# A three-block transformer forward pass: order of the first loads and splits, and identity products in TensorE's foreseen waits

## The chip, the core and the metric

The kernel runs on one core of a Trainium2 chip. The metric is the device time of one execution in microseconds (us), shown as the median of several runs. TensorE is the matrix engine (PE in the profile, PEld for its weight loads), VectorE is DVE, ScalarE is ACT, GpSimd is POOL, and SyncE (SP) issues most transfers.

## What is computed

The input x has 256 tokens of 2048 features, all in float32. A first block is a mixture of three mixers, cross attention to 256 memory tokens, and a feed-forward part with a short convolution; a second part has two layers. In outline:

```python
proj = h @ w_in                      # split into s5, stick-breaking and sparse-attention inputs
y = concat(s5_mixer(u5), stick_breaking(sq, sk, sv), nsa_mixer(nq, kc, vc, ksl, vsl, ksw, vsw, g))
h = layer_norm(ALPHA * h + y @ w_out)
h = layer_norm(ALPHA * h + memory_cross_attention(h, mem))
h = layer_norm(ALPHA * h + conv_ffn(h))
...
# second part, two layers
x = x + mixer(rmsnorm(x))            # latent attention and pooling, then a short convolution
x = x + square(relu(rmsnorm(x) @ w_mlp_up)) @ w_mlp_down
```

Nearly all the arithmetic is in products of a 256-token activation with weight matrices that are read once from memory. The change concerns the very first of them, `h @ w_in`, and the places where TensorE waits.

## The kernel before, in words

**Main products.** `plan` is a list of entries. An entry is a group of weights, mostly 4 rows of 128 by 512 columns (1 MB), loaded by SP into one of three buffers `raw`. To keep float32 precision, each weight group is split in two halves of 1024 columns: ScalarE writes the rounded part to `whi` (`split_hi`), VectorE the rest to `wlo` (`split_lo`). The activation is split in the same way into a tile `rt` of 512 columns, high part and low part for 256 tokens. TensorE then does one product of `whi` with all 512 columns, and one of `wlo` with 256, for each 128 by 128 block of weights (`blocks`). The results land in PSUM tiles called `bank`. Small tensors of the mixers live in one large tile `ft` (some in `st`), cut into buffers by `buf`.

**Order of work.** The program text of each engine is written in Python by a planner. The main products are emitted in the order of `plan`; side work (transposes, set-up of the mixers, attention heads, normalisation) is written as generators ("threads") that the planner advances between the main products. It does so by a clock of its own: `spent` adds the planned cost of each operation to a clock per engine (`clk`), and keeps for each 32-column block of a tile the planned time of the last write and the last read (`region`). A thread is advanced when its time has come by the planned TensorE clock. `B.side(gen, t)` adds a thread with a due time `t` in ns; `turn_cols` has 40000 and the set-up of the sparse attention (`nsa.setup`) 45000. `copy_out`, `scale_rows` and `vt` choose an engine by these clocks, and `Arena.get` the place of a buffer.

**The start.** `network` emits the first loads. `load_consts` loads all constants (1004 columns, identity first) from ACT's queue. The loop over four chunks of x (256 tokens by 512 features each, 0.5 MB) loads chunk 0 from SP's queue and chunks 1 to 3 from ACT's, and weight groups 0 to 2 from SP's. A one-column copy on POOL reads chunk 2, and POOL's own loads and its chain of small operations for the S5 mixer stand behind that copy. Then `load_cols` issues some fifteen small loads of parameter columns from SP's queue; the next weight group is loaded by SP after these. `run` first splits two half groups (`self.ahead(2)`); `start`, called before the first entry, adds the threads, among them `trans` for the four chunks: it transposes each 128-feature piece on TensorE and splits it with ScalarE and VectorE into an `rt` tile.

**Names.** `identr` is a 128 by 128 identity in the rounded format; it serves already to add terms to a bank (`extra` in `blocks`). `mixfree` is the list of banks that side work may take; the main products have banks of their own (`lin`).

Of the kernel before, what the change touches and what calls it, by code (L numbers as in the profile page):

```python
# [70 lines left out]
CBIG, COFF, COH = _consts()  # L71
# [10 lines left out]
NCOL = _o  # L82
# [18 lines left out]
DEPTH = 6  # L101
MARGIN = 0.0
ORDER = "u5 sq sk kv nq0 nq1 g sv h0 h1 ksl units ksw"
W = "waits"
READ = "read"

# [146 lines left out]
class Builder:  # L253
# [5 lines left out]
    def __init__(self, tc, I, out):  # L259
        self.tc, self.I, self.out = tc, I, out  # L260
        self.nc = Engines(tc.nc, self)
        self.clk = dict(pe=0.0, dve=0.0, act=0.0, pool=0.0, qsync=0.0, qact=0.0, qpool=0.0, dma=0.0)
        self.times = {}
        self.table = None
        self.cur = None
        self.plan = []
        self.queue = []
        self.depth = DEPTH
        self.spawned = []
        self.persist = 0  # L270
        self.evacs, self.reading = None, {}
        self.quiet = 0


    def act(self, out, in_, func=AF.Copy, scale=1.0, bias=0.0, accum=None):
# [122 lines left out]
    def bank(self):  # L398
        while not self.mixfree:
            yield W  # L400
        return self.mixfree.popleft()

    def keep_bank(self, has=lambda: False):

        while not has() and (not self.mixfree or self.persist >= max(1, 8 - self.nlin - 2)):
            yield W
        if has():
# [29 lines left out]
    def spent(self, key, name, a, kw):  # L437
        outs = [kw[k] for k in ("out", "accum_out") if kw.get(k) is not None] or [a[0]]
        ins = [x for x in list(a) + list(kw.values()) if hasattr(x, "shape") and hasattr(x, "dtype") and not any(x is o for o in outs)]
        n = max([_free(x) for x in outs + ins])  # L440
        pointers = sum(_free(x) == 1 for x in ins) if n > 1 else 0
        end = LAT
        if name == "dma_start":
            if key == "pool":

                self.clk["pool"] += 1000.0
                self.clk["qpool"] = max(self.clk["qpool"], self.clk["pool"] + 1000.0)

            key, c = "q" + key, 450.0
            size = max(outs[0].shape[0], ins[0].shape[0]) * n * 4 / 360.0  # L450
        elif key == "pe":
            end = 60.0
            c = _free(outs[0])
            if name == "transpose":
                c = 0.84 * c
            elif ins[-1].dtype == FR:
                c = c / 2.4 + 14.1
            else:
                c = max(c * 1.667, 26)
        elif key == "act":  # L460
            c = 92 + 0.84 * n + 93 * pointers
            s = TABLE.get(kw.get("func"))
            if s and s != self.table:
                self.table = s
                c += 1300.0
        elif key == "pool":
            c = 120 + 3.5 * n if name == "tensor_copy" else 150 + (0.74 if name == "affine_select" else 2.1) * n
        elif name in ("tensor_scalar", "tensor_copy"):
            c = 64 + 0.52 * n + 62 * pointers
        else:  # L470
            c = 66 + 1.05 * n * (8 if name == "reciprocal" and n > 16 else 1) + 60 * pointers
        t = self.clk[key]
        ri = [x for x in map(self.region, ins) if x is not None]
        ro = [x for x in map(self.region, outs) if x is not None]
        for w, r in ri:
            t = max(t, w.max())
        for w, r in ro:
            t = max(t, r.max(), 0 if key == "pe" or name == "dma_start" else w.max())
        self.clk[key] = t + c
        self.lastc = c  # L480
        if name == "dma_start":
            self.clk["dma"] = max(self.clk["dma"], t + 1000) + size
            c, end = self.clk["dma"] - t, 1500.0
        f = t + c + end
        for w, r in ri:
            np.maximum(r, f - 60, out=r)
        for w, r in ro:
            w[:] = f
        if self.cur is not None:
            self.cur.t = max(self.cur.t, f)  # L490

    def ready(self, ap):
        return self.region(ap)[0].max()

    def step(self, th):

        was, self.cur = self.cur, th
        try:
            r = next(th.gen) or True
            th.steps = 99 if r is READ else th.steps + (r is not W)  # L500
            return r
# [250 lines left out]
    def run(self):  # L752
        self.halves = [(i, j) for i, e in enumerate(self.plan) for j in range(e.nhalf)]
        self.nhi = self.nlo = self.nhalf = 0
        self.ahead(2)
        for i, e in enumerate(self.plan):
            for f in e.before:
                f()
            self.consume(i)
        self.flush()  # L760
# [38 lines left out]

    def load_consts(self):  # L800
        nc = self.nc
        self.cb = self.buf(CBIG.shape[1], True)
        nc.scalar.dma_start(out=self.cb.ap, in_=self.I["cbig"])
        nc.vector.tensor_copy(out=self.identr, in_=self.cst("ident"))
        self.ones = self.buf(128, True)
        nc.vector.memset(self.ones.ap, 1.0)
        self.small = self.buf(8)
        for i, v in enumerate((1.0 / 2048, 1.0 / 512, 1.0 / 192, 1.0 / 1536, math.pi / 2)):
            nc.vector.memset(self.small.ap[:, i:i + 1], v)
        self.halfpi = self.small.ap[:, 4:5]  # L810
        nc.vector.memset(self.small.ap[:, 5:7], 0.0)
        for h in range(2):
            nc.vector.memset(self.small.ap[h * 64:h * 64 + 64, 5 + h:6 + h], 1.0 / 192)
# [5 lines left out]
    def load_cols(self):  # L819

        nc = self.nc
        self.pcol = self.buf(NCOL, True)
        nt = (NCOL + 127) // 128
        st = self.buf(nt * 128)
        sv = st.v(nt)
        for name, rows in COLS:
            src = self.I[name]
            names = " ".join(f"a{i}" for i in range(len(src.shape)))
            flat = src.rearrange(f"{names} -> ({names})") if len(src.shape) > 1 else src
            flat = flat.rearrange("(r c) -> r c", c=128)  # L830
            r = 0
            while r < rows:
                g = COL0[name] + r
                t, p = divmod(g, 128)
                m = min(rows - r, 128 - p)
                nc.sync.dma_start(out=sv[p:p + m, t], in_=flat[r:r + m])
                r += m
        def turn():
            for t0 in (0, 4):
                b = yield from self.bank()  # L840
                n = min(512, NCOL - t0 * 128)
                for t in range(t0, min(t0 + 4, nt)):
                    m = min(128, NCOL - t * 128)
                    nc.tensor.transpose(b[:, (t - t0) * 128:(t - t0) * 128 + m], sv[0:m, t], self.cst("ident")[0:m, 0:m])
                yield
                self.act(self.pcol.ap[:, t0 * 128:t0 * 128 + n], b[:, 0:n])
                self.unbank(b)
                yield
            st.free()
            self.hb = self.buf(4)  # L850
            c = COL0["s5_b_glu"]
            self.ts(self.hb.ap, self.pcol.ap[:, c:c + 4], 0.5, ALU.mult)
            yield
        self.turn_cols = turn
# [1658 lines left out]
def block1(B, dpool):  # L2513
    nc, I = B.nc, B.I
# [9 lines left out]
    stg = {}  # L2524

    def stage(n, c):
        stg[n, c] = B.buf(1024)
        (nc.scalar if n == "x" and c else nc.sync).dma_start(out=stg[n, c].v(2), in_=I[n][0, :, c * 512:(c + 1) * 512].rearrange("(t p) f -> p t f", p=128))
        return stg[n, c]

    def trans(n, c, lin=False):
# [30 lines left out]
    RT = 0.9  # L2562

    def start():
        B.side(s5.setup())
        for c in range(4):
            B.side(trans("x", c), B.ready(stg["x", c].ap))
        B.side(B.turn_cols(), 40000.0)
        B.side(nsa.setup(), 45000.0)
# [94 lines left out]
    def units():  # L2664
        B.side(nsa.biases(), prio=2)
        for h in range(16):
            for br in range(2):
                B.side(nsa.unit(h, br), prio=3)
    for n in ORDER.split():
        if n == "units":  # L2670
# [268 lines left out]
def network(tc, I, out, es):  # L2939
    B = Builder(tc, I, out)  # L2940
    nc = B.nc
    dpool = es.enter_context(tc.tile_pool(name="dr", bufs=1, space=bass.MemoryType.DRAM))
    B.setup(es)
    B.load_consts()
    stage, s5, nsa, e = block1(B, dpool)
    block2(B, e)
    s5.load_rows()
    for c in range(4):
        x = stage("x", c)
        if c < B.NRAW:  # L2950
            B.load(c)
        if c == 2:

            t = B.buf(1)
            nc.gpsimd.tensor_copy(out=t.ap, in_=x.ap[:, 0:1])
    s5.load()
    nsa.load()
    B.load_cols()
    B.negones = B.buf(128)
    nc.vector.memset(B.negones.ap, -1.0)  # L2960
    gen_setup(B)
    B.run()
    return B
# [27 lines left out]
```

## Time and profile before

| | us |
|---|---|
| median of 3 runs | 3513.49 |
| the runs | 3511.28 to 3513.76 |
| profiled execution, whole | 3515.05 |
| its span, first to last instruction | 3513.3 |
| TensorE busy in the span | 3426.3 (98%) |
| VectorE busy | 2371.4 (67%) |
| ScalarE busy | 1725.5 (49%) |
| GpSimd busy | 215.7 (6%) |
| mean granted TensorE clock | 0.989 of full speed |

A busy TensorE is not always one at its peak: its products overlap and their ends are modelled. The granted clock has two levels, 1.00 (2.4 GHz) and 0.50 (1.2 GHz); a value between them is a mean over a stretch that has both. All instructions that the planner emits through its wrappers carry one line number, L233, so groups are told apart by the tiles they write and read.

### The profile page before, as it was taken

How to read it: one execution, taken by the hardware profiler on the slowest of the kernel's cores; microseconds unless marked ns; L12 is line 12 of the kernel's file. 1: busy time of each engine (PE TensorE's matmuls, PEld its weight loads, DVE VectorE, ACT ScalarE, POOL GpSimd, SP SyncE). 2: the span in 40 equal slices, each digit the busy share in tenths (PEclk: the TensorE clock that was granted, in tenths of full speed). 3: DMA queues.
4: the chain of work that ended last, by engine and by line, in shares of the span. 5: the costliest groups of instructions: out<-in, count | busy, mean ns of one | idle time of the engine just before them, and what ended most of it. 6: DMA issues, size and time to landing. Idle time of an engine off the chain costs nothing.

```text
span 3513.3 us, 49562 instructions
## 1 busy us (share of the span) xinstructions
PE 3426.3 (98%) x19448; PEld 2940.8 (84%) x19448; DVE 2371.4 (67%) x3978; ACT 1725.5 (49%) x2652; POOL 215.7 (6%) x319
## 2 busy tenths in 40 slices
PE   8998999899999999999999999999999999999999
PEld 6777688788888887787888888888888888888887
DVE  4977677876676578877765656567666664656565
ACT  4445645555455455654544444444454544434343
POOL 4001010001000001000000000000221000000001
PEclk8999999999999999999999999999999999999999
DMA  5452244355555555443555555555555555555554
GB/s 181 132 166 96 56 168 165 134 192 188 187 191 192 187 186 167 150 126 126 170 190 192 188 186 189 192 180 192 184 189 191 192 191 186 187 191 192 186 187 143
DMA packets 323779, 605.15 MB, mean 172 GB/s; under 512 B 18843, under 2 KB 36243, under 8 KB 323545
## 3 DMA queue, kind: packets, MB, share of 16 engines
q1 hardware_dynamic: 319609, 596.91, 51.5%
q10 hardware_dynamic: 3264, 4.19, 0.5%
q8 instruction: 152, 2.49, 0.3%
q0 software_dynamic: 672, 0.89, 0.1%
q14 instruction: 82, 0.67, 0.1%
HBM read 599.26 MB, written 2.69 MB: 171 GB/s over the span
## 4 chain that ended last, share of the span: by engine, by line
PE 87%; DVE 10%; issue 1%; ACT 1%; POOL 1%; DMA 1%; ACTq 0%; SPq 0%; DVEq 0%; POOLq 0%
PE bank L233 87%; DVE ft L233 6%; DVE wlo L233 3%; POOL ft L233 1%; DVE rt L233 0%; ACT ft L233 0%; DMA ft<-in_x_dram 0%; ACT whi L233 0%; DMA raw<-in_w_in_dram 0%; DMA raw<-in_even_w_ukv_dram 0%; DMA raw<-in_even_w_uq_dram 0%; POOL st L233 0%; DVE st L233 0%; ACT rt L233 0%; ACT L284 0%
## 5 line engine op out<-in xcount | busy, mean ns | idle before, releaser
L233 PE MATMUL bank<-rt,whi 128*128 128x512 f32 (+1 forms) x8784 | 2785.7, 399 | 47.6 <-DVE ft L233 27.3
L233 PEld LDWEIGHTS bank<-rt,wlo 128*128 128x128 f32 (+1 forms) x8784 | 1651.7, 189 | 388.8 <-DVE wlo L233 0.4
L233 DVE TENSOR_TENSOR wlo<-raw,whi 128x1024 fp32r<-128x1024 f32 x1134 | 1379.2, 1222 | 719.6 <-ACT whi L233 717.1
L233 ACT ACTIVATE whi<-raw 128x1024 fp32r<-128x1024 f32 x1134 | 1189.4, 1050 | 1344.3 <-PE bank L233 1271.5
L233 PE MATMUL bank<-rt,wlo 128*128 128x256 f32 (+1 forms) x8784 | 1727.8, 279 | 0.0
L233 PEld LDWEIGHTS bank<-rt,whi 128*128 128x128 f32 (+1 forms) x8784 | 1347.6, 189 | 79.6 <-DVE ft L233 28.9
L233 DVE TENSOR_TENSOR ft<-bank,ft 128x256 f32<-128x256 f32 (+2 forms) x879 | 358.3, 420 | 286.7 <-ACT ft L233 198.5
L233 POOL TENSOR_TENSOR ft<-ft 128x256 f32<-128x256 f32 (+1 forms) x179 | 149.1, 844 | 2912.8 <-DVE ft L233 2061.4
L233 ACT ACTIVATE ft<-bank 128x256 f32<-128x256 f32 (+3 forms) x499 | 190.4, 392 | 189.7 <-PE bank L233 161.1
L233 PE MATMUL bank<-ft 128*128 128x128 f32 (+9 forms) x1073 | 213.5, 346 | 33.9 <-DVE ft L233 21.8
L233 DVE SCALAR_TENSOR_TENSOR ft<-ft 128x256 f32<-128x256 f32 (+2 forms) x441 | 225.8, 513 | 13.0 <-ACT ft L233 2.5
L233 PEld LDWEIGHTS bank<-ft 128*128 128x128 f32 (+4 forms) x1073 | 137.6, 171 | 87.6 <-DVE ft L233 25.4
L233 ACT ACTIVATE ft<-ft 128x256 f32<-128x256 f32 (+3 forms) x365 | 165.8, 467 | 90.4 <-DVE ft L233 70.1
L233 DVE TENSOR_TENSOR ft<-ft 128x256 f32<-128x256 f32 (+4 forms) x463 | 194.1, 442 | 14.1 <-ACT ft L233 8.7
L233 ACT ACTIVATE rt<-ft 128x256 fp32r<-128x256 f32 x317 | 138.6, 439 | 85.2 <-DVE ft L233 80.3
L233 DVE TENSOR_TENSOR rt<-ft,rt 128x256 fp32r<-128x256 f32 x220 | 91.7, 445 | 5.2 <-ACT rt L233 5.2
L233 PE MATMUL bank<-whi,rt 128*128 128x256 f32 (+1 forms) x320 | 80.6, 329 | 1.4 <-DVE ft L233 1.4
L233 ACT ACTIVATE ft<-ft,st 128x256 f32<-128x256 f32 (+1 forms) x146 | 64.5, 464 | 19.3 <-DVE st L233 18.5
L233 PEld LDWEIGHTS bank<-whi,rt 128*128 128x128 f32 x320 | 55.5, 190 | 7.6 <-ACT whi L233 1.2
L233 PE MATMUL bank<-wlo,rt 128*128 128x256 f32 (+1 forms) x160 | 52.1, 326 | 0.0
L233 DVE SCALAR_TENSOR_TENSOR rt<-ft,rt 128x256 fp32r<-128x256 f32 x97 | 45.1, 475 | 0.3 <-ACT rt L233 0.3
L233 ACT ACTIVATE rt<-bank 128x256 fp32r<-128x256 f32 x56 | 20.0, 380 | 45.0 <-PE bank L233 44.9
(76 smaller groups left out, 464.9 us busy)
## 6 DMA issues: line engine op xcount, KB each, us to landing
raw<-in_w_mlp_up_dram SPq DMA_DIRECT2D x128, 1024.0 KB, 5.3
raw<-in_w_mlp_down_dram SPq DMA_DIRECT2D x128, 1024.0 KB, 5.1
raw<-in_ffn_w_up_dram SPq DMA_DIRECT2D x88, 1024.0 KB, 5.0
raw<-in_odd_w_in_dram SPq DMA_DIRECT2D x48, 1024.0 KB, 5.2
raw<-in_ffn_w_down_dram SPq DMA_DIRECT2D x44, 1024.0 KB, 5.1
raw<-in_w_in_dram SPq DMA_DIRECT2D x36, 1024.0 KB, 5.1
raw<-in_w_out_dram SPq DMA_DIRECT2D x16, 1024.0 KB, 5.1
raw<-in_even_w_in_dram SPq DMA_DIRECT2D x16, 1024.0 KB, 5.4
```

The lines of the kernel that those rows point to most:

```text
L233: return f(*a, **kw)
```

## The change

1. Constants: only the identity (128 columns) is loaded first, from ACT's queue; the other 876 columns follow from SP's queue after chunk 2 of x and weight group 2. All four chunks of x are loaded from SP's queue.
2. Splits: `self.ahead(2)` moves from `run` into `start`, behind the transposes and splits of chunk 0, which are emitted at once and not as a thread.
3. Buffers: the constants, the parameter columns and the one-column buffer get widths that are multiples of 32.
4. `warm`: when the planner's clock says that TensorE will wait 1400 ns or more for the operands of its next operation (`KEEP`), products of the identity with itself, 128 by 512, are emitted ahead of that operation, one for each 227 ns of the foreseen wait less 600 ns (`KEPT`). They write the first bank of `mixfree` whose planned use has ended; where there is none, none is emitted. The planner's clocks don't count them.

```diff
@@ -101,6 +101,9 @@
 DEPTH = 6
 MARGIN = 0.0
 ORDER = "u5 sq sk kv nq0 nq1 g sv h0 h1 ksl units ksw"
+
+KEEP = 1400.0
+KEPT = 600.0
 W = "waits"
 READ = "read"
 
@@ -270,6 +273,7 @@
         self.persist = 0
         self.evacs, self.reading = None, {}
         self.quiet = 0
+        self.peend, self.nwarm = 0.0, 0
 
 
     def act(self, out, in_, func=AF.Copy, scale=1.0, bias=0.0, accum=None):
@@ -476,6 +480,9 @@
             t = max(t, w.max())
         for w, r in ro:
             t = max(t, r.max(), 0 if key == "pe" or name == "dma_start" else w.max())
+        if key == "pe":
+            self.warm(t)
+            self.peend = t + c
         self.clk[key] = t + c
         self.lastc = c
         if name == "dma_start":
@@ -488,6 +495,19 @@
             w[:] = f
         if self.cur is not None:
             self.cur.t = max(self.cur.t, f)
+
+    def warm(self, t):
+
+        gap = t - self.peend
+        if gap < KEEP or self.peend == 0:
+            return
+        old = [b for b in self.mixfree if max(x.max() for x in self.region(b)) <= self.peend]
+        if not old:
+            return
+        x = self.identr.unsqueeze(1).to_broadcast([128, 4, 128])
+        for _ in range(int((gap - KEPT) / 227.0)):
+            self.tc.nc.tensor.matmul(old[0].rearrange("p (a b) -> p a b", a=4), lhsT=self.identr, rhs=x, start=True, stop=True)
+            self.nwarm += 1
 
     def ready(self, ap):
         return self.region(ap)[0].max()
@@ -752,7 +772,6 @@
     def run(self):
         self.halves = [(i, j) for i, e in enumerate(self.plan) for j in range(e.nhalf)]
         self.nhi = self.nlo = self.nhalf = 0
-        self.ahead(2)
         for i, e in enumerate(self.plan):
             for f in e.before:
                 f()
@@ -799,8 +818,9 @@
 
     def load_consts(self):
         nc = self.nc
-        self.cb = self.buf(CBIG.shape[1], True)
-        nc.scalar.dma_start(out=self.cb.ap, in_=self.I["cbig"])
+        self.cb = self.buf(1024, True)
+
+        nc.scalar.dma_start(out=self.cb.ap[:, 0:128], in_=self.I["cbig"][:, 0:128])
         nc.vector.tensor_copy(out=self.identr, in_=self.cst("ident"))
         self.ones = self.buf(128, True)
         nc.vector.memset(self.ones.ap, 1.0)
@@ -819,7 +839,7 @@
     def load_cols(self):
 
         nc = self.nc
-        self.pcol = self.buf(NCOL, True)
+        self.pcol = self.buf((NCOL + 31) // 32 * 32, True)
         nt = (NCOL + 127) // 128
         st = self.buf(nt * 128)
         sv = st.v(nt)
@@ -2525,7 +2545,7 @@
 
     def stage(n, c):
         stg[n, c] = B.buf(1024)
-        (nc.scalar if n == "x" and c else nc.sync).dma_start(out=stg[n, c].v(2), in_=I[n][0, :, c * 512:(c + 1) * 512].rearrange("(t p) f -> p t f", p=128))
+        nc.sync.dma_start(out=stg[n, c].v(2), in_=I[n][0, :, c * 512:(c + 1) * 512].rearrange("(t p) f -> p t f", p=128))
         return stg[n, c]
 
     def trans(n, c, lin=False):
@@ -2562,8 +2582,10 @@
     RT = 0.9
 
     def start():
+        now(trans("x", 0))
+        B.ahead(2)
         B.side(s5.setup())
-        for c in range(4):
+        for c in range(1, 4):
             B.side(trans("x", c), B.ready(stg["x", c].ap))
         B.side(B.turn_cols(), 40000.0)
         B.side(nsa.setup(), 45000.0)
@@ -2950,9 +2972,10 @@
         if c < B.NRAW:
             B.load(c)
         if c == 2:
-
-            t = B.buf(1)
-            nc.gpsimd.tensor_copy(out=t.ap, in_=x.ap[:, 0:1])
+            nc.sync.dma_start(out=B.cb.ap[:, 128:CBIG.shape[1]], in_=I["cbig"][:, 128:])
+
+            t = B.buf(32)
+            nc.gpsimd.tensor_copy(out=t.ap[:, 0:1], in_=x.ap[:, 0:1])
     s5.load()
     nsa.load()
     B.load_cols()
```

## Rows read from the trace of the kernel before

**Rows 1.** Page, part 1: busy time, share of the span and instructions, of TensorE.

```profile
PE 3426.3 (98%) x19448; PEld 2940.8 (84%) x19448; DVE 2371.4 (67%) x3978; ACT 1725.5 (49%) x2652; POOL 215.7 (6%) x319
```

**Rows 2.** Windows: busy us (instructions) by engine, PE clock, DMA share, GB/s.

```profile
0.00:17.20 17.20, 2.77 (x11) 1.92 (x12) 4.70 (x21) 4.22 (x7) 6.63 (x14) 1.00 0.88 319
...
7.00:10.00 3.00, 0.68 (x4) 0.29 (x3) 0.51 (x4) 0.00 (x0) 0.00 (x0) 1.00 1.03 383
...
100.00:200.00 100.00, 95.40 (x496) 74.85 (x496) 97.66 (x197) 42.04 (x63) 6.67 (x8) 0.98 0.42 135
...
700.00:1340.00 640.00, 640.00 (x3677) 558.42 (x3676) 438.07 (x600) 340.87 (x489) 45.83 (x51) 1.00 0.56 189
...
1715.00:3430.00 1715.00, 1715.00 (x9855) 1496.70 (x9854) 1062.42 (x1442) 794.57 (x1057) 64.46 (x60) 1.00 0.57 189
```

**Rows 3.** Waits of TensorE from 85 us on: total us, times, longest.

```profile
PE bank L233 <- DVE ft L233: 44.1, 47, 5.9
PE bank L233 <- DVE rt L233: 18.6, 10, 6.4
```

**Rows 4.** Timeline of the start: start us, us, engine, work [idle before <-releaser].

```profile
11.84 2.00 ACT L233 ACTIVATE whi<-raw 128x1024 fp32r<-128x1024 f32 x2 [7.15 <-DMA raw<-in_w_in_dram]
...
12.43 0.19 POOL L233 COPY st<-ft 128x1 f32<-128x1 f32 x1 [9.45 <-DMA ft<-in_x_dram]
...
17.23 1.22 PE L233 MATMUL bank<-rt,whi 128*128 128x512 f32 x2
...
26.59 9.88 SPq L233 DMA_DIRECT2D raw<-in_w_in_dram  x4
...
31.70 1.06 ACT L233 ACTIVATE whi<-raw 128x1024 fp32r<-128x1024 f32 x1 [2.28 <-DMA raw<-in_w_in_dram]
...
42.90 0.91 PE L233 MATMUL bank<-ft 33*128 33x383 f32 x2 [1.48 <-DVE ft L233]
```

**Rows 5.** Groups of TensorE instructions from 17 to 42.5 us: count, busy us, mean ns.

```profile
L233 PE MATMUL bank<-rt,whi 128*128 128x512 f32 x52 | 17.8, 422 | 1.2 <-DVE rt L233 1.2
```

**Rows 6.** Windows of stretches around waits, columns as in the other windows.

```profile
44.00:67.50 23.50, 23.50 (x91) 21.25 (x91) 8.85 (x23) 6.38 (x16) 9.37 (x32) 0.50 0.24 71
...
129.00:132.50 3.50, 3.50 (x12) 2.59 (x11) 3.47 (x8) 1.06 (x1) 0.00 (x0) 0.53 0.00 0
...
180.00:190.00 10.00, 6.85 (x35) 4.96 (x34) 9.90 (x21) 3.38 (x7) 0.00 (x0) 1.00 0.85 252
...
308.00:312.00 4.00, 4.00 (x17) 2.32 (x14) 2.12 (x6) 2.15 (x6) 0.79 (x2) 0.50 0.17 60
...
316.00:320.50 4.50, 4.49 (x14) 3.63 (x15) 3.85 (x8) 3.26 (x8) 2.03 (x8) 0.52 0.27 51
...
348.00:355.00 7.00, 6.54 (x25) 5.84 (x26) 3.17 (x12) 6.37 (x11) 3.15 (x7) 0.54 0.01 2
...
1404.00:1409.00 5.00, 4.70 (x15) 4.02 (x16) 5.00 (x10) 3.92 (x8) 0.00 (x0) 0.50 0.00 0
...
1581.00:1587.00 6.00, 6.00 (x20) 5.09 (x21) 5.78 (x17) 4.54 (x9) 0.00 (x0) 0.52 0.73 262
```

**Rows 7.** Timeline of TensorE at waits, identity products and low clock.

```profile
127.51 0.73 PE L233 MATMUL bank<-rt,whi 128*128 128x512 f32 x2 [1.45 <-DVE ft L233]
...
185.17 0.73 PE L233 MATMUL bank<-rt,whi 128*128 128x512 f32 x2 [3.15 <-DVE ft L233]
...
348.46 1.97 PE L233 MATMUL bank<-ft 128*128 128x128 f32 x6 [5.87 <-DVE ft L233]
...
633.42 0.63 PE L233 MATMUL bank<-rt,identr 128*128 128x512 f32 x2
...
651.82 1.05 PE L233 MATMUL bank<-rt,whi 128*128 128x512 f32 x2
...
1578.23 0.47 PE L233 MATMUL bank<-rt,whi 128*128 128x512 f32 x1 [1.74 <-DVE ft L233]
```

**Rows 8.** Groups of TensorE instructions from 44 to 67.5 us.

```profile
L233 PE MATMUL bank<-st,ft 33*128 33x16 f32 x60 | 13.2, 372 | 0.0
```

## The prediction

> **What bounds the kernel now.** I read the page first: TensorE is busy 98% of the span [rows 1], so only what lets its order of work finish sooner counts. The windows then show where nothing can be won. From 700 to 1340 and from 1715 to 3430 TensorE is busy throughout, at full clock, with the other engines well below it [rows 2]. That is 2355 of 3513 us, and the change removes no work there. What is left is the time before 700 and the time from 1340 to 1715.
>
> The waits of TensorE after 85 us are nearly all for VectorE: 44.1 us for ft tiles and 18.6 us for rt tiles [rows 3]. The timeline shows three kinds of loss. First, the main products begin at 17.23 [rows 4]. Second, thirteen waits after that last 1.4 us or more, from 42.90 (1.48) to 1578.23 (1.74) [rows 4, 7]. Third, after many of them the granted clock is near 0.50, the lower level: the longest such stretch is 44 to 67.5 [rows 6]. A pair of 512-column products takes 1.05 us there, against 0.63 for a pair of the same width at full clock [rows 7].
>
> **The first loads.** Today the x chunks and the constants leave ACT's queue while x0 and the weights leave SP's; they share the transfer engines, and the first weight group is split only from 11.84 [rows 4]. The mean rate from 0 to 17.2 is 319 GB/s and from 7 to 10 it is 383 [rows 2]. So 17.2 us moved 5.49 MB, which takes 14.3 us at 383; the dead time ahead is 2.9 us. After the change, 64 KB of ident, 0.52 MB of x0 and 1.05 MB of weights stand ahead: 1.64 MB, 4.3 us, landed at 7.2. ScalarE's first half split (half of the 2.00 us pair [rows 4]) ends at 8.2, and x0's transposes and splits, emitted first, fit before it. The first main product can start at about 8.5, which is 8.7 us sooner. That is the upper bound of this edit; the lower is 0.
>
> Three things stand in its way. (a) SP's queue: the x chunks (1.57 MB) and the rest of the constants (0.45 MB) now stand ahead of the column loads and of the fourth weight group, which SP issues at 26.59 today [rows 4]. At 383 GB/s these are at worst 5.3 us. ScalarE splits that group at 31.70, ending 32.8 [rows 4]. TensorE has 52 main high products by 42.5 [rows 5]; 48 of them are the first three groups, so the fourth begins four products before the last, near 39.9. The slack is 7.1 us, which covers either the delay or most of the gain, not both. (b) POOL: its copy behind chunk 2 waits until 12.43 [rows 4]. After the change 3.74 MB stand up to chunk 2, 2.9 + 9.8 = 12.7: unchanged. So the S5 setup that follows on POOL starts as before, VectorE's part comes after it, and the product at 42.90 still waits for VectorE [rows 4]. What TensorE can keep is the main work that the planner moves ahead of that product. (c) The planner places this side work by its own clock (due times 40000 and 45000 ns), which also starts sooner, so part moves ahead. I take 4 us, about the middle of 0 and 8.7. After 67.5 VectorE reaches 97.66 us in 100 [rows 2], but what feeds that stretch is TensorE's chain from 42.90 on, so I let the 4 us through.
>
> The other moves cost nothing that the path sees. ScalarE loses three issues; `B.buf(32)` copies the same one column. The wider buffers align the blocks by which the planner tracks dependencies, so its clocks and the order of side work change everywhere. I cannot price that by row. I take 0, and as bounds a tenth either way of the 62.7 us of waits for VectorE after 85 [rows 3]: 6 us.
>
> **The identity products.** Each writes 512 columns; the same form with identr as the moving tile exists in the normalisation step and takes 0.63 us for an overlapped pair, where the low clock has 1.05 for a main pair [rows 7]. The price of one comes from the long stretches: 2355 us for 13532 products, half of 512 columns and half of 256 [rows 2], are 0.174 us in the mean, so 0.23 for 512 columns. If the planner foresees the thirteen waits as they are, they are 38.7 us together, and less 0.6 us each, at one product for each 227 ns, that makes about 130: some 30 us of TensorE time, all inside waits and ending some 0.6 us before the end of each. Cost: 0 while the wait covers them. Without that cover it is 0.23 us each, or 0.46 at half the clock, and all TensorE work behind them is late. I charge 1 us for misjudged waits; bounds 0 and 30.
>
> What they can give back is (1 minus the granted clock) times the stretch, and only where TensorE sets the pace [rows 6]:
> - 44 to 67.5, 0.50: up to 11.8 us. But 13.2 us of it are 60 tiny products 33x16 [rows 8], and the clock did not return while they ran between short bursts of main work. Identity products sit ahead, not inside. I take 3 of 0 to 11.8.
> - 308 to 312 and 316 to 320.5: up to 2.0 + 2.2. ScalarE and POOL steps lie between. I take 2.
> - 348 to 355, after the 5.87 us wait [rows 7]: up to 3.2; VectorE is busy only 3.17 of 7 us. I take 3.
> - 1581 to 1587: up to 2.9, after three short waits that the planner may not foresee. I take 1.5.
> - 1404 to 1409, and the like place at 650: up to 2.5 each. But VectorE is busy 5.00 of 5 us: it makes the operands, and a faster TensorE waits for the next one. I take 0.5 for both together. From 129 to 132.5, where the clock is 0.53, VectorE is busy 3.47 of 3.5 us: nothing, of up to 1.6.
>
> The rows do not make the length of a wait alone decide: after the 1.45 us wait at 127.51 the clock fell to 0.53 on average, around the 3.15 us wait before 185.17 it stayed at 1.00 [rows 6, 7]. The Trainium skill, TensorE: Matmul & The Clock Gate, section "HAM oscillation — how this bites in real kernels", makes only longer idle stretches dangerous; by it the shorter waits need no filling. The trace disagrees at 127.51.
>
> **Sum.** -4 (loads) -3 -2 -3 -1.5 -0.5 (clock) +1 (misjudged) = -13 us. The profiled execution took 3515.05 us (span 3513.3), so 3502 by it; it stands 1.6 us above the median of the runs, 3513.49, from which the sum gives 3500.5. I say 3501. A measurement tells 0.2% from no change: 7 us, so 3506.5 and 3520.5 are the borders.
>
> **Rivals.**
> 1. *More is recovered.* The clock stays up through 44 to 67.5 and the loads bring 6.4: -6.4 -11.8 -4.2 -3.2 -2.9 = -28.5, so 3485. For it: no wait falls inside that stretch, so the fall may hang on the 1.48 us wait alone. Against: the tiny products. Chance 0.12.
> 2. *The start is absorbed.* The main work starts at 8.5, and the product of 42.90 still waits for POOL and VectorE, at the same place in the order; the wait there grows by what was won. Then -10 + 1 = -9 at best, and where VectorE's pace eats the early clock terms too (-3, -2), -4: 3509. For it: POOL's unchanged 12.43. Against: due times that move main work ahead. Chance 0.10.
> 3. *The products do not do it.* The planner foresees few waits, finds no idle bank, or the clock falls all the same: -4 alone, 3509. Chance 0.07.
> 4. *Only long waits matter.* As a mechanism here: the clock terms behind waits over 3 us stay (-2 and -3), the others are 0: -4 -5 +1 = -8, near 3506 to 3507, which I count as no change. The rule is the one of the page named above. Chance 0.05, since 127.51 speaks against it.
> 5. *Slower: products where there is no wait.* The planner foresees waits that the chip does not have, in stretches where TensorE sets the pace (between the waits of 348.46 and 1578.23, say). Each such product delays everything behind it by 0.23 us. The 14 us won otherwise are gone at 61 of them; with 92 in excess the kernel takes 3521. For it: waits of the planner are not those of the trace, and the blocks change. Against: the two long stretches without a wait suggest that its clock is close. Chance 0.13.
>
> My forecast has 0.53. Faster is that and rival 1: 0.65. Within 0.2%: rivals 2, 3 and 4: 0.22. Slower: 0.13. The range: below 3482 I leave rival 1 with a good reordering, under 0.1; the upper end takes in rivals 2 to 4 with the reordering's spread, 3517, leaving most of rival 5 out. For the forecast alone 3491 to 3506.
>
> **What would show it.** Right: x0's transposes and splits ahead of the first weight split, which starts near 7 to 8 us; first main products before 10; some 130 products bank<-identr, in the waits; full clock at the places of 308, 348 and 1581; TensorE's total of waits for VectorE about the same or filled. Wrong: a new wait for the fourth weight group near 30 us; a longer wait at the product of 42.90; products where the trace before shows TensorE busy; the low clock still there from 44; or waits moved by the new order of side work by more than 6 us.

## The result and the profile after

The changed kernel takes 3533.89 us, median of 4 runs (3530.56 to 3540.45), against 3513.62 (3511.28 to 3515.06) for the kernel before on the same chip. The ratio is 1.0061, with a 95% interval of 1.0048 to 1.0074: slower by about 20 us, where 12 us less was forecast. The profiled execution took 3532.09 us (span 3530.4). Its mean granted clock is higher than before, 0.993 against 0.989.

Page, part 1, of the kernel after:

```profile
PE 3467.3 (98%) x19665; PEld 2973.1 (84%) x19665; DVE 2376.4 (67%) x3980; ACT 1735.4 (49%) x2651; POOL 221.7 (6%) x321
```

TensorE has 217 more instructions than in [rows 1] and 41 us more busy time. The groups of TensorE by line name them: all 217 are identity products. (Line numbers shift with the edit: L233 of the kernel before is L236 here, and L509 is the product in `warm`.)

```profile
L509 PE MATMUL bank<-identr 128*128 128x512 f32 x217 | 55.2, 402 | 0.7 <-DVE ft L236 0.7
```

Waits of TensorE from 85 us on, after (total us, times, longest):

```profile
PE bank L236 <- DVE ft L236: 29.3, 43, 2.9
PE bank L236 <- DVE rt L236: 10.1, 7, 4.5
PE bank L236 <- ACT ft L236: 4.5, 6, 2.3
```

The waits for VectorE are 39.4 us, against the 62.7 of [rows 3]. The same order without the products has 77.7 (r1 below), so the products do fill waits. Yet the kernel is longer than before: these totals alone say nothing of the time.

Timeline of the start, after:

```profile
5.50 1.94 PE L236 MATMUL bank<-ft 128*128 128x128 f32 x8 [5.50 <-DMA ft<-in_x_dram]
...
8.36 2.00 ACT L236 ACTIVATE whi<-raw 128x1024 fp32r<-128x1024 f32 x2 [0.50 <-DMA raw<-in_w_in_dram]
...
9.47 1.22 PE L236 MATMUL bank<-rt,whi 128*128 128x512 f32 x2 [2.03 <-ACT whi L236]
...
42.85 0.73 PE L236 MATMUL bank<-rt,whi 128*128 128x512 f32 x2 [1.33 <-DVE ft L236]
...
47.18 1.20 PE L236 MATMUL bank<-ft 33*128 33x383 f32 x2 [1.74 <-DVE ft L236]
```

The first weight split starts at 8.36 instead of 11.84, and the first main products at 9.47 instead of 17.23 [rows 4]. The set-up product of the sparse attention, at 42.90 before and just ahead of the low clock, now comes at 47.18 with a wait of 1.74 us.

Windows of the kernel after:

```profile
44.00:67.50 23.50, 21.76 (x95) 18.42 (x94) 10.86 (x31) 5.72 (x14) 8.73 (x36) 0.65 0.24 71
...
700.00:1340.00 640.00, 640.00 (x3677) 558.42 (x3676) 435.58 (x596) 336.69 (x476) 43.29 (x47) 1.00 0.56 190
1715.00:3430.00 1715.00, 1713.07 (x9838) 1494.41 (x9837) 1067.28 (x1460) 801.75 (x1067) 64.64 (x60) 1.00 0.58 188
```

The long stretches are as in [rows 2]; the loss lies outside them. To place it I use a yardstick that is the same in every kernel here: VectorE's 1134 low-part splits `wlo<-raw`. The start of the n-th split (counted from 0) in one trace less its start in the trace before tells where a kernel stands; each trace is one execution. For the kernel after: -3.7 us at split 40 (180 us before), +2.5 at split 56 (232), +29.6 at 60 (254), +49.8 at 76 (306), +13.1 at 92 (463), +17.6 at 300 (1094), +17.4 at 1130. So the early gain was there, and was lost from 180 us on: 6.2 us up to split 56, 10.6 more up to 92 and 4.5 more up to 300. The middle one stands between 232 and 463 us. The swing to +49.8 and back is partly side work moved ahead of these splits.

What stands there, in the timeline of TensorE after:

```profile
244.55 4.47 PE L509 MATMUL bank<-identr 128*128 128x512 f32 x19
248.96 3.78 PE L236 MATMUL bank<-ft,raw 128*128 128x60 f32 x32
...
255.70 8.91 PE L509 MATMUL bank<-identr 128*128 128x512 f32 x38
...
266.05 3.52 PE L236 MATMUL bank<-ft 128*32 128x256 f32 x18 [0.89 <-DVE ft L236]
270.25 3.47 PE L509 MATMUL bank<-identr 128*128 128x512 f32 x14 [0.69 <-DVE ft L236]
...
277.82 3.68 PE L236 MATMUL bank<-ft,raw 128*128 128x60 f32 x32
```

and in that of before:

```profile
243.65 7.25 PE L233 MATMUL bank<-ft,raw 128*128 128x60 f32 x64
```

The two groups of 32 products `ft,raw` 128x60 are the hidden layers h0 and h1 of the sparse attention's compression. Before, they stand back to back, all 64. After, they are 28.9 us apart, and between them TensorE does products of the S5 mixer (128x256), which wait for VectorE, and 52 identity products.

### The profile page after: what moved, and what is told of

Same layout as the page of the kernel before. It is cut to its first block, busy times and chain, and to the rows that moved or that the text cites. A ratio compares the mean times of both kernels' runs of the same rounds, so it can differ in the third digit from the quotient of the medians.

```text
span 3530.4 us, 49956 instructions
## 1 busy us (share of the span) xinstructions
PE 3467.3 (98%) x19665; PEld 2973.1 (84%) x19665; DVE 2376.4 (67%) x3980; ACT 1735.4 (49%) x2651; POOL 221.7 (6%) x321
## 4 chain that ended last, share of the span: by engine, by line
PE 88%; DVE 7%; ACT 1%; issue 1%; DMA 0%; POOL 0%; SPq 0%; DVEq 0%; ACTq 0%
PE bank L236 88%; DVE ft L236 5%; DVE wlo L236 2%; ACT ft L236 0%; DVE rt L236 0%; ACT whi L236 0%; PE bank L509 0%; POOL ft L236 0%; DMA raw<-in_even_w_out_dram 0%; DMA raw<-in_even_w_uq_dram 0%; ACT L236 0%; ACT rt L236 0%; ACT L288 0%; SPq L236 0%; DVEq L236 0%
## 5 line engine op out<-in xcount | busy, mean ns | idle before, releaser
L236 PE MATMUL bank<-rt,whi 128*128 128x512 f32 (+1 forms) x8784 | 2784.4, 399 | 33.8 <-DVE ft L236 25.1
L236 PEld LDWEIGHTS bank<-rt,wlo 128*128 128x128 f32 (+1 forms) x8784 | 1650.8, 188 | 390.9 <-DVE wlo L236 3.1
L236 DVE TENSOR_TENSOR wlo<-raw,whi 128x1024 fp32r<-128x1024 f32 x1134 | 1380.1, 1221 | 750.7 <-ACT whi L236 744.7
L236 ACT ACTIVATE whi<-raw 128x1024 fp32r<-128x1024 f32 x1134 | 1189.5, 1051 | 1358.1 <-PE bank L236 1307.8
L236 PE MATMUL bank<-rt,wlo 128*128 128x256 f32 (+1 forms) x8784 | 1728.2, 279 | 1.3 <-DVE wlo L236 1.3
L236 PEld LDWEIGHTS bank<-rt,whi 128*128 128x128 f32 (+1 forms) x8784 | 1347.0, 189 | 65.5 <-DVE ft L236 31.1
L236 DVE TENSOR_TENSOR ft<-bank,ft 128x256 f32<-128x256 f32 (+1 forms) x879 | 358.8, 420 | 260.1 <-ACT ft L236 176.4
L236 POOL TENSOR_TENSOR ft<-ft 128x256 f32<-128x256 f32 (+1 forms) x181 | 155.3, 870 | 2915.7 <-DVE ft L236 2060.8
L236 ACT ACTIVATE ft<-bank 128x256 f32<-128x256 f32 (+4 forms) x498 | 192.2, 390 | 166.7 <-PE bank L236 163.2
L236 DVE SCALAR_TENSOR_TENSOR ft<-ft 128x256 f32<-128x256 f32 (+2 forms) x441 | 226.7, 515 | 11.4 <-ACT ft L236 1.6
L236 PE MATMUL bank<-ft 128*128 128x128 f32 (+10 forms) x1073 | 207.9, 337 | 23.1 <-DVE ft L236 6.9
L236 ACT ACTIVATE ft<-ft 128x256 f32<-128x256 f32 (+3 forms) x365 | 165.7, 467 | 97.9 <-DVE ft L236 74.9
L236 DVE TENSOR_TENSOR ft<-ft 128x256 f32<-128x256 f32 (+4 forms) x461 | 197.8, 452 | 15.9 <-ACT ft L236 10.6
L236 PEld LDWEIGHTS bank<-ft 128*128 128x128 f32 (+5 forms) x1073 | 133.9, 165 | 76.4 <-issue 19.5
L236 ACT ACTIVATE rt<-ft 128x256 fp32r<-128x256 f32 x317 | 139.3, 441 | 103.3 <-DVE ft L236 94.9
L236 DVE TENSOR_TENSOR rt<-ft,rt 128x256 fp32r<-128x256 f32 x220 | 93.6, 445 | 2.3 <-ACT rt L236 2.3
L236 PE MATMUL bank<-whi,rt 128*128 128x256 f32 (+1 forms) x320 | 80.6, 330 | 0.0
L236 ACT ACTIVATE ft<-ft,st 128x256 f32<-128x256 f32 (+1 forms) x143 | 63.7, 466 | 19.3 <-DVE st L236 17.3
L236 PEld LDWEIGHTS bank<-whi,rt 128*128 128x128 f32 x320 | 55.5, 189 | 5.7 <-issue 0.8
L509 PE MATMUL bank<-identr 128*128 128x512 f32 x217 | 55.2, 402 | 0.7 <-DVE ft L236 0.7
L236 PE MATMUL bank<-wlo,rt 128*128 128x256 f32 (+1 forms) x160 | 52.1, 326 | 0.0
L509 PEld LDWEIGHTS bank<-identr 128*128 128x128 f32 x217 | 40.6, 192 | 9.1 <-DVE ft L236 1.3
```

The lines of the kernel that those rows point to most:

```text
L236: return f(*a, **kw)
L509: self.tc.nc.tensor.matmul(old[0].rearrange("p (a b) -> p a b", a=4), lhsT=self.identr, rhs=x, start=True, stop=True)
```

## Experiments

Each run has a median, and a ratio to the kernel before on the same chip with a 95% interval. Three theories go through most of the first twelve runs: P, the identity products delay TensorE where there was no wait; O, the wider buffers changed the planner's order and opened the hole between h0 and h1; R, the widths cost in many places.

**r1, the change without products.**

```diff
-KEEP = 1400.0
+KEEP = 1e12
```

> The changed kernel without the identity products; loads, widths and with them the order of all other work stay as changed. Theory P (products where the chip had no wait: 217 of them at 0.23 us are 50 us, and 71 stand between 244 and 274 us): most of the loss goes, 3503 to 3512 us. Theory O (the wider buffers changed the planner's order, so that the two hidden-layer entries of the compression stand 29 us apart with nothing else for TensorE between them): the loss stays, 3525 to 3545 us, the waits of TensorE rise from 57.6 us by some 40 us, and more low clock than in the changed kernel.

3548.12 us, 1.0099 (1.0084 to 1.0114). P falls: without the products the kernel is 14 us slower. The loss stays, as O has it, 3 us above O's range. Nearly all of the difference arises in the hole: r1 is 12.0 us behind the kernel after at split 60, 13.9 at 64, 13.9 at 92. The window of the hole, r1:

```profile
240.00:282.00 42.00, 26.33 (x92) 16.39 (x90) 27.99 (x66) 10.71 (x16) 0.00 (x0) 0.61 0.20 71
```

and the kernel after:

```profile
240.00:282.00 42.00, 39.32 (x210) 29.77 (x209) 30.52 (x71) 18.29 (x29) 1.99 (x4) 1.00 0.19 66
```

The clock is 0.61 without and 1.00 with the products.

**r2, the products alone on the kernel before** (`KEEP`, `KEPT` and `warm` of the change, nothing else).

> The kernel before with the identity products alone; loads and widths as before, so the order of all other work is that of before. Theory P: slower, 3520 to 3540 us. Theory O: the products stand in waits that are there, 3500 to 3514 us, with the clock mean above 0.989.

3513.11 us, 1.0001 (0.9992 to 1.0011), with 161 products. Windows of r2, at the places of [rows 6]:

```profile
308.00:312.00 4.00, 3.92 (x28) 2.92 (x28) 2.31 (x7) 3.52 (x8) 0.79 (x2) 1.00 0.30 104
316.00:320.50 4.50, 4.50 (x15) 3.30 (x15) 3.58 (x8) 2.19 (x6) 2.10 (x8) 0.50 0.31 60
348.00:355.00 7.00, 5.54 (x21) 4.99 (x22) 4.16 (x14) 6.93 (x15) 2.96 (x6) 0.52 0.00 0
...
1404.00:1409.00 5.00, 3.89 (x18) 2.79 (x17) 5.00 (x15) 4.68 (x9) 0.00 (x0) 1.00 0.01 3
1581.00:1587.00 6.00, 5.75 (x28) 4.47 (x27) 5.97 (x11) 4.39 (x10) 0.00 (x0) 1.00 1.01 378
```

The clock came back at 308, 1404 and 1581, and no time with it. At 308 the next wait took it: TensorE waits 2.64 us for GpSimd at 314.74, against 0.81 at 316.01 before. And some products stand where nothing waits. In r2:

```profile
632.86 3.14 PE L508 MATMUL bank<-identr 128*128 128x512 f32 x13
635.84 1.07 PE L235 MATMUL bank<-rt,whi 128*128 128x512 f32 x4
```

and before, where the same main products follow at once:

```profile
632.50 1.09 PE L233 MATMUL bank<-rt,whi 128*128 128x512 f32 x4
```

From split 141 to 142 (654 us) r2 goes from 0.5 to 3.2 us behind, and r10 below loses as much there.

**r3, the three widths alone on the kernel before.**

```diff
-        self.cb = self.buf(CBIG.shape[1], True)
+        self.cb = self.buf(1024, True)
...
-        self.pcol = self.buf(NCOL, True)
+        self.pcol = self.buf((NCOL + 31) // 32 * 32, True)
...
-            t = B.buf(1)
+            t = B.buf(32)
```

> The kernel before with the three buffer widths rounded up to multiples of 32 and nothing else (all constants still in one load, no products). Theory O: the hole between the two hidden-layer entries is there, 3525 to 3545 us. Theory P: the widths move no time that can be measured, 3507 to 3520 us.

3538.71 us, 1.0071 (1.0056 to 1.0086): not one load, product or copied column differs, and it is 25 us slower. The hole is there, with a wait of 8.79 us for VectorE at 263.51. **r4, the new loads and splits alone** (the change without products and with the old widths):

> The changed kernel with the old buffer widths and without the products: only the first loads and splits in their new order. Both theories: the start gives about 3.5 us, as the two traces show up to 200 us, and no hole: 3504 to 3514 us. If it is slower than 3520 us, the loads alone turn the order for the worse and theory O puts the cause in the wrong edit.

3522.99 us, 1.0029 (1.0018 to 1.0040): not the 3504 to 3514 that both theories gave. h0 and h1 stand together; the loss comes later (-7.1 us at split 76, +8.4 at 92). That 25 and 10 make the 35 of r1 is no proof that the parts add up: two of the three widths cost 31 and 21 us by themselves (r11 and r12 below).

**r5, the hole put into the kernel before**, by letting the planner hold h1's entry back until 15 of the 16 slices of S5 are done.

```diff
-        e.before.append(lambda: B.wait_for(lambda: j in nsa.G))
+        e.before.append(lambda: B.wait_for(lambda: j in nsa.G and (j == 0 or sum(s5.ycnt) >= 15)))
```

> The kernel before (its widths, loads and no products) with one wait added to the planner: the second hidden-layer entry is emitted only when 15 of the 16 S5 slices are done. This puts 13 groups of S5 products between the two hidden-layer entries, as the changed order has. Theory O (that hole is the cost of the widths): 3528 to 3545 us, the main work late by 30 to 55 us from 250 us on, some given back at the later S5 wait. Rival theory R (the widths cost in many places, the hole is given back in full): 3509 to 3519 us.

3540.97 us, 1.0076 (1.0059 to 1.0093). Level with before up to split 56 (+0.1), +26.7 at 92, +27.3 at the end. The hole in r5's timeline:

```profile
243.74 3.67 PE L233 MATMUL bank<-ft,raw 128*128 128x60 f32 x32
...
259.24 1.06 PE L233 MATMUL bank<-ft 128*32 128x256 f32 x2 [9.78 <-DVE ft L233]
...
273.57 1.06 PE L233 MATMUL bank<-ft 128*32 128x256 f32 x2 [7.74 <-DVE ft L233]
...
279.09 7.08 PE L233 MATMUL bank<-ft,raw 128*128 128x60 f32 x32
```

**r6 and r7** shrink the hole in r1: r6 plans `ksl` ahead of `h0 h1` in `ORDER`, r7 sets `DEPTH` to 7.

> The changed kernel without products (3548 us) and with the ksl projection planned ahead of the two hidden-layer entries, which closes the hole with main work. Theory O: 3515 to 3530 us, main work no longer late at 260 to 300 us. Theory R: 3540 to 3555 us.

> The changed kernel without products (3548 us) and with seven side threads under way instead of six: the two hidden-layer entries stand next to each other again, as in the kernel before. Theory O: 3510 to 3530 us. Theory R: 3540 to 3555 us.

3528.72 us, 1.0048 (1.0033 to 1.0063), and 3532.43 us, 1.0056 (1.0041 to 1.0071): 16 to 19 us better than r1. From the start of h0 to that of h1 it is 37.4 us in r1, 17.6 in r6 and 6.0 in r7. r6 lies in O's range; r7, with the hole all but closed, is 2 us above it. The hole is enough for a loss of this size (r5), and with a smaller one about half of r1's 35 us goes; the rest stays.

**r8, r4 with the products.**

> The changed kernel with the old three widths: new loads and splits, and the products, without the hole. If products give back only what a low clock takes: the loads alone take 3523 us with 18 us of low-clock loss in 298 to 480, of which the products return about a third, 3514 to 3520 us. If the products bring nothing as on the order of before: 3521 to 3526 us.

3524.89 us, 1.0033 (1.0020 to 1.0046): no better than r4's 1.0029. The products pay only where there is a hole.

**r9, the new loads in the order of before**: the transfers of the change, but the planner's books (its clocks and its planned times of each block) are told of the old ones, so every engine's order of work stays. The splits stay where they were. **r10, the same with the products.**

```diff
-        nc.scalar.dma_start(out=self.cb.ap, in_=self.I["cbig"])
+        self.spent("act", "dma_start", (), dict(out=self.cb.ap, in_=self.I["cbig"]))
+        self.tc.nc.scalar.dma_start(out=self.cb.ap[:, 0:128], in_=self.I["cbig"][:, 0:128])
...
+        B.spent("act" if n == "x" and c else "sync", "dma_start", (), kw)
+        B.tc.nc.sync.dma_start(**kw)
...
+            tc.nc.sync.dma_start(out=B.cb.ap[:, 128:], in_=I["cbig"][:, 128:])
```

> The kernel before with the new loads (identity first, all x chunks and the rest of the constants from SP's queue), but the planner's books filled as before, so that every engine's order of work is that of the kernel before; splits stay where they were. If the loss of the loads alone (3523 us) lies in the order that the planner makes of them: 3508 to 3514 us, the start 2 to 4 us sooner and some of it eaten by the later waits. If it lies in the transfers themselves: 3519 to 3526 us.

> The same with the identity products, on the order of the kernel before. The products gave nothing on that order (3513.1 against 3513.3 us), so: as r9 within 3 us. If the products can use the earlier start: 3500 to 3507 us.

r9: 3509.82 us, 0.9992 (0.9983 to 1.0001). r10: 3512.58 us, 1.0002 (0.9993 to 1.0010). So r4's loss was order, in which I count the moved splits, and not transfers. But the gain of r9 is not that of the start: it is 3.5 us ahead at split 0, level at splits 4 and 8 (+0.3, 0.0), and 4.8 ahead from split 12 to the end. Timeline of TensorE in r9:

```profile
19.22 1.12 PE L233 MATMUL bank<-ft 128*128 128x128 f32 x4 [2.95 <-DMA ft<-in_x_dram]
...
42.89 0.91 PE L233 MATMUL bank<-ft 33*128 33x383 f32 x2 [1.19 <-DVE ft L233]
```

and its window behind:

```profile
44.00:67.50 23.50, 23.50 (x118) 21.01 (x118) 13.51 (x32) 8.00 (x18) 9.37 (x32) 0.71 0.30 85
```

In the old order the transposes of x's last chunk stand in TensorE's queue where they did, and now wait 2.95 us for their load at 19.22: most of the 3.5 us. The set-up product comes at 42.89, as at 42.90 before. What is kept lies behind it, where the clock is 0.71 instead of 0.50.

**r11, the width of `pcol` alone; r12, the width of POOL's one-column buffer alone.**

> The kernel before with the one width of the parameter columns, 584 to 608 columns; no instruction changes but the order that the planner makes. Its two hidden-layer entries have 4 groups of S5 products between them, where the kernel with all three widths has 15. Theory O (what stands between them sets the price): 3516 to 3530 us. Theory R (the widths cost in many places by their number): 3513 to 3522 us.

> The kernel before with the one-column buffer of POOL's copy taken 32 columns wide; the order changes in many places, but the two hidden-layer entries stay side by side. Theory O: 3506 to 3520 us. If any change of the order costs: 3520 us and more.

r11: 3543.11 us, 1.0088 (1.0075 to 1.0102). r12: 3533.46 us, 1.0058 (1.0044 to 1.0072). r11 is above both of its ranges. r12 is above O's and lies where the theory that any change of the order costs had put it, which the nudges below contradict. I had sized r11's hole by the four groups between h0 and h1; the timeline of r11 shows that few groups can wait long:

```profile
249.26 7.08 PE L233 MATMUL bank<-ft,raw 128*128 128x60 f32 x32 [7.49 <-DVE ft L233]
256.27 3.94 PE L233 MATMUL bank<-ft 128*32 128x256 f32 x16
279.41 7.08 PE L233 MATMUL bank<-ft,raw 128*128 128x60 f32 x32 [19.20 <-DVE ft L233]
```

That is the same hole, 26.7 us of waiting. r12 has none: it is 2.5 us behind at split 76 and 14.3 at 92, so there is a second place, 306 to 463 us.

**r13 to r16, nudges.** One planner constant each on the kernel before, no width, load or operation: `SIDE` 2500 to 2400, `MARGIN` 0 to 20, `EARLY` 400 to 420, `LAT` 130 to 140.

> The kernel before with one constant of the planner nudged: SIDE 2500 to 2400 (how far ahead side work is taken). No load, buffer or operation changes; the order of side work does, from about a tenth of the program on. Theory N (the order of before is at the low end of many; any change of the planner's books costs 5 to 35 us where the sequence between 240 and 470 us is redrawn): 3518 to 3548. Theory W (only wider buffers cost, because they take away false dependencies that spaced the side work well; a nudge that keeps the blocks costs nothing): 3506 to 3518.

> The kernel before with MARGIN 0 to 20 (a thread counts as ready 20 ns later). Theory N: 3518 to 3548. Theory W: 3506 to 3518.

> The kernel before with EARLY 400 to 420. The order first differs later than in the other nudges. Theory N: 3518 to 3548, or nothing if the stretch from 240 to 470 us keeps its waits. Theory W: 3506 to 3518.

> The kernel before with LAT 130 to 140 (the planned latency from an operation's end to its reader, 10 ns more). The order differs from the first transposes on. Theory N: 3518 to 3548. Theory W: 3506 to 3518.

3510.88 us, 0.9996 (0.9986 to 1.0005); 3531.23, 1.0049 (1.0033 to 1.0066); 3517.78, 1.0014 (1.0004 to 1.0023); 3512.61, 0.9996 (0.9987 to 1.0006). N and W both fall as put: a nudge need not cost, and r14 costs 18 us without a wider buffer. In all four h0 and h1 stand together; r14 loses at the second place. Windows from split 76 to 92, before:

```profile
305.98:462.90 156.92, 147.79 (x814) 108.12 (x815) 101.03 (x367) 102.46 (x273) 28.06 (x55) 0.93 0.22 67
```

r14:

```profile
308.81:478.86 170.05, 152.79 (x816) 112.13 (x814) 101.87 (x368) 101.76 (x270) 26.09 (x55) 0.91 0.21 61
```

The work of VectorE and ScalarE is the same; TensorE is idle 17.3 us (170.05 - 152.79) instead of 9.1, and the lower clock takes the rest. The waits are not the same in each: in r14 they are for GpSimd (8.3 us) and ScalarE (6.9), in r12 mostly for VectorE (13.2). r4 (172.4 us) and r12 (168.8) look like r14, r13 (158.0) and r15 (155.1) like before.

r16 shows what the stretch from 44 on can give. Its timeline and window:

```profile
46.18 0.91 PE L233 MATMUL bank<-ft 33*128 33x383 f32 x2 [0.47 <-DVE ft L233]
...
49.31 3.52 PE L233 MATMUL bank<-st,ft 33*128 33x16 f32 x30
```

```profile
44.00:67.50 23.50, 23.03 (x141) 20.11 (x140) 16.03 (x35) 8.66 (x17) 9.06 (x33) 0.93 0.49 154
```

More main work stands ahead of the set-up product, its wait is 0.47 us, and the kernel is 12.8 us ahead at split 12. It keeps 9.9 of them at split 92 and 7.4 at the end of that execution, one of the two shortest of ten; the median keeps 0.2.

**r17, r16 with the loads of r9; r18, that with the products.**

> The order of r16 (LAT 140) with the new loads, which the planner's books don't see (as in r9). In r16 the set-up product of the sparse attention waits 0.47 us at 46.18, and the stretch 44 to 67.5 keeps a granted clock of 0.90 to 0.96, 13 us better than before at the thirteenth split. Theory C (an earlier start is kept because the main work of this order reaches further): about 3 us less than r16, 3507 to 3510. Theory A (absorbed: that product waits for POOL's and VectorE's chain, whose start has not moved; the wait grows by what the start won, and the low clock comes back): 3510 to 3520, with a wait of 2 us or more there and a clock nearer 0.50 behind it.

> r17 with the identity products of the change. Theory C: what waits there are after the loads are filled and the clock is held, 3503 to 3509. Theory A, or products that win nothing where VectorE paces (as in r2 and r10): the same as r17 within 3 us.

3511.09 us, 0.9996 (0.9988 to 1.0005), and 3514.46 us, 1.0004 (0.9995 to 1.0013). r17 is 3.5 us ahead at split 0 and level by split 4, as r9; then it is r16 again (-13.0 at split 12). The time lies in A's range, 1 us above C's, and its interval reaches into both. The trace speaks against C: nothing of the start is kept. A is right on the absorbing, but not on its place: the start goes into the same wait for x (3.03 us at 19.28), not into one at the set-up product, and the low clock did not come back (0.85). In r18 the planner foresaw a wait that r17 does not have. r17:

```profile
46.04 0.91 PE L233 MATMUL bank<-ft 33*128 33x383 f32 x2
```

r18:

```profile
45.84 3.14 PE L508 MATMUL bank<-identr 128*128 128x512 f32 x13
48.91 0.91 PE L235 MATMUL bank<-ft 33*128 33x383 f32 x2
```

Thirteen products put that product 2.9 us later, and at split 24 r18 is 2.9 us behind r17 (-9.3 against -12.2). The median is 3.4 us above r17's, just outside A's 3 us; the two intervals overlap, so that the products cost is shown at this place and not by the whole time.

## Why the prediction was wrong

Two steps failed. The larger is the one priced as "I take 0, and as bounds a tenth either way of the 62.7 us": the new order of side work. r1 stands 35 us above before, and the loads can't have cost that: r9, with the same transfers in the old order, loses nothing. Each alone costs: the widths 25 us (r3), the loads with the moved splits 10 (r4). With the products, which win 14 back, some 20 are left. The bound was taken from the waits that the trace of before shows. But the order could make waits that were not there: 26.7 us in r11 before h0 and h1, with a clock of 0.54 from 240 to 286. The step's own words, that clocks and order "change everywhere", asked for a bound as wide as the largest move of a chain, not a tenth of today's waits.

The smaller is the price of a clock that comes back, -10 in the sum. r10 has the new loads and the products in the old order, so only the moved splits and the order term are missing from it: -13 by the sum, and 3512.58 us against 3512.54 as measured. Even in the old order the forecast gain does not come.

- *Loads, -4.* In the order of the change, -3.5 to -3.7 at splits 36 to 40: the size agrees, which may be luck, for a new order alone moves these splits too (r3 -0.6 and -2.0, r16 -14.5 and -17.1). Where the loads left the order as it was (r9, r17) the earlier start is gone by split 4. That is rival 2's absorption, but in a wait for x's last chunk and not at the product of 42.90. r9's 4.8 us stand behind that product, where the clock is higher. Even that is not clearly the loads' doing: r13, without them, has a set-up product with the wait of before and the same 0.71.
- *SP's queue and POOL.* Nearly as argued: TensorE shows no wait for the fourth weight group, and the set-up product still waits for VectorE. POOL's copy comes at 13.81, 1.4 us later than the 12.43 before.
- *Clock from 44 on, -3 of 11.8.* The products did not reach it (0.50 in r2; 0.58 in r1 and 0.65 after, where the order moved). The tiny products were wrongly written off: a group of thirty takes 3.52 us in r16 where [rows 8] has 13.2 for both, so the whole stretch is worth about 13 us. r16 had no products and more main work ahead of the set-up product; what kept its clock up was not isolated.
- *Clock at 308, 348, 1404 and 1581, -7.* At 316 and 348 it stayed low in r2: the 5.87 us wait before 349.46 has no product in it. At the others the clock came back and won nothing: r2 is level with before (0.6 us behind at split 92, 2.4 at the end). For 1404 I had said why, VectorE is busy 5.00 of 5 us; at 1581 it is 5.97 of 6 in r2, and its 5.78 of 6 in [rows 6] should have had the same answer. At 308 VectorE is busy 2.31 of 4; there the wait for GpSimd at 314.74 grew by 1.8 us.
- *Misjudged products, +1.* 217 instead of 130, at 55.2 / 217 = 0.25 us instead of 0.23. In the new order they are a net gain of 14 us (r1), in four orders without the hole they gain nothing (r2, and r8, r10, r18 beside r4, r9, r17). Rival 5 had the right sign by the wrong mechanism: products without a wait exist (2.7 us in r2 and r10, 2.9 in r18), but they are not what made the change slower.

Shown: the hole between h0 and h1 is enough for some 27 us (r5), and it is in the change, r1, r3 and r11. Shown: a second place, 306 to 463 us, costs 12 to 16 us in r4, r12 and r14. Open: how much of the change's 20 us is the hole, since no run closes it with the products in, and r7, which all but closes it without them, is still 20 us slower than before. Part of that comes late: r1, r3, r6 and r7 each lose 7 to 8 us behind split 92. Open too: which dependency of the attention units makes the second place, and whether widths lose more than other redrawings. Three width changes (all three, and two of them singly) cost 21 to 31 us, four nudges -2 to +18; that is too few to tell. The moved splits and the width of the constants were not run alone. No kernel here is clearly faster than before; r9 comes nearest, 0.9992 with an interval that reaches 1.0001.

## What to carry to other kernels

Where a planner writes the order of work, an edit that touches its books is two edits: price the redrawn order first, by running the edit with the books unchanged and the books changed without the edit. Bound such a term by the longest wait that a moved chain could make, not by the waits that the tuned order still has. Before filling waits to hold a clock, look which engine is at 100% in the stretch behind: where it was not TensorE, a higher clock only made TensorE wait here (r2).

## What the runs showed of the hardware

- The set-up product's wait alone does not fix the clock behind it: 1.48 us before gave 0.50 over 44 to 67.5, 1.49 us in r13 gave 0.71, 0.47 us in r16 gave 0.93. In r16 the granted clock is 1.00 from 44 to 53.5, through that wait and thirty tiny products, and 0.50 from 54.2 to 57.5: a pair of 512 columns takes 1.06 us at 54.39 and 55.67, and 0.63 from 57.91 on. Behind the second thirty, at 59.41, it stays 1.00. The Trainium skill, TensorE: Matmul & The Clock Gate, section "A second HAM failure mode: psum-queue depth-cycling", tells of a clock that falls where TensorE idles often and briefly between groups of products; TensorE is busy 9.03 of the 9.5 us ahead of this fall, the rest being the one wait, so no run here shows that it is such a case. The rule of long idle stretches that the prediction weighed does not fit this fall either. What made the clock fall stays open.
- Thirty products 33x16 take 6.58 us before, at a granted clock of 0.50, and 3.52 us in r16 at 1.00.
- Executions of one kernel lie up to 11 us apart (r16: 3507.65 to 3518.72; its profiled one 3507.74, its median 3512.61). A difference of a few us between the ends of two profiles is no result; a step between two neighbouring splits that a second kernel repeats says more.
